# Four subtractions per pair of weight blocks, moved from VectorE to GpSimd in a Strassen-type MLP of a two-layer decoder trunk

## The chip, the cores and the metric

The kernel runs on 1 core of one Trainium2 chip. The metric is the device time of one execution in microseconds, as the median of 3 runs.

## What is computed

The reference is a decoder trunk with two layers over 1024 positions and 1024 channels, all in float32. Each layer has a mixer (a gated recurrence with a state-space layer in layer 0, latent attention in layer 1) and then a gated MLP with a short causal convolution. The change lies in the MLP:

```python
def conv_ffn(hn, w_in, conv_w, conv_b, w_out):
    a, u = jnp.split(hn @ w_in, 2, axis=-1)
    a = lax.conv_general_dilated(a, conv_w[:, None, :], window_strides=(1,),
                                 padding=[(CONV_W - 1, 0)],
                                 dimension_numbers=('NWC', 'WIO', 'NWC'),
                                 feature_group_count=D_FF) + conv_b
    return (jax.nn.silu(a) * u) @ w_out

for layer in range(DEPTH):          # DEPTH = 2
    ...                             # the mixer
    h = h + conv_ffn(rmsnorm(h, norm_ffn_g[layer]), ffn_w_in[layer], ffn_conv_w[layer],
                     ffn_conv_b[layer], ffn_w_out[layer])
```

D_FF is 2816, so `w_out` is 2816 x 1024.

## The kernel before

Both products of the MLP use a Strassen-type scheme: seven products of blocks where a plain product needs eight, paid for by sums of blocks. Each float32 product is made of three matmuls on a high and a low part of its operands (`mm3`, lines 161 to 165). `split` (lines 128 to 132) makes the two parts: ScalarE copies the high one, VectorE subtracts it from the source.

**Up-projection** (`ffn`, lines 823 to 1114). The 2816 columns come in 22 blocks of 128, f = 0 to 21; each is a `Pair` (of a block of the gate and one of the value). Per pair there are seven products, run in the order a11, s2, a12, s3, s1, a22, s4 (line 1071), each of 12 matmuls. They go into three PSUM banks X, Y and Z. The products s2, s3 and a22 go one after the other into Y, and between two of them VectorE reads Y: line 915 after s2, line 919 after s3, line 929 after a22. Line 936 reads Z after s4. GpSimd makes the sums s1 to s4 of the weights (lines 884 to 890), adds the upper half of the convolution's input (line 902) and multiplies half of the result (line 938). ScalarE copies p1 and p5 out of the banks (lines 909 and 924). The convolution (lines 1122 and 1124) is on VectorE and its silu on ScalarE (line 1125). The loads of the weights are issued three steps ahead (`LOOK`, `prep`), from SyncE's queue.

**Sums for the down-projection.** After every second pair (`tail`, line 934), two kinds of small jobs are appended to a list, `later`. `row_sums` (lines 956 to 974) makes four sums of the MLP's rows for the pair. `weight_sums` (lines 976 to 992) makes four sums of the quarters of two blocks of 128 rows of `w_out`: it loads the two blocks (line 982), waits three jobs, subtracts four times (line 987), and after each subtraction stores the result in the DRAM tile `t_dram` (line 988). `TURNS` (line 46) says how many such turns follow which pair: one after pairs 5, 7, 11, 15 and 19, two after 9, 13 and 17, so 11 per layer. Both kinds of jobs work in the same two buffers, `homes()` (lines 950 to 954). One job is taken from the list after each product, two if more than 14 are left (lines 1100 to 1102). The down-projection (`down`) reads `t_dram` (line 1158).

The order of the instructions on each engine is not written out by hand: a planner sets it from modelled durations when the program is built. Only TensorE's order in the two projections is fixed, by `issue_after` (lines 862 and 1173). Each engine works through its own queue in order, so that an instruction that waits holds all that stand behind it in that queue.

Of the kernel before, what the change touches and what calls it, by code (L numbers as in the profile page):

```python
# [17 lines left out]
ALU = mybir.AluOpType  # L18
# [39 lines left out]
class Trunk:  # L58
# [764 lines left out]
    def ffn(self, L, h, pool, final=None):  # L823
# [3 lines left out]
        V, G, ACT = nc.vector, nc.gpsimd, nc.scalar  # L827
# [122 lines left out]
        def homes():  # L950
            return (
                self.const.tile([P, S], F32, tag="gain", name="q1", bufs=1),
                self.w.tile([P, S], F32, tag=f"wlo{WBUFS - 1}", name="q2", bufs=1),
            )
# [21 lines left out]
        def weight_sums(q):  # L976

            x = []

            def load():  # L980
                for i, y in enumerate(homes()):
                    nc.sync.dma_start(out=y, in_=w_out[(2 * q + i) * P:(2 * q + i + 1) * P])
                    x.extend((y[:, lo], y[:, hi]))

            def step(i, out, a, b):
                def go():
                    V.tensor_tensor(out=x[out], in0=x[a], in1=x[b], op=ALU.subtract)
                    nc.sync.dma_start(out=t_dram[q, i], in_=x[out])
                return go

            wait = lambda: None
            return [load, wait, wait, wait, step(0, 0, 1, 0), step(2, 1, 3, 1), step(1, 3, 3, 0), step(3, 2, 2, 3), wait]
# [692 lines left out]
```

## Time and profile before

| | us |
|---|---|
| median of 3 runs | 2261.92 (2260.53 to 2264.37) |
| the profiled execution | 2260.85 |
| its span, first to last instruction | 2259.1 |
| TensorE busy | 2192.1 (97%) |
| VectorE busy | 1661.3 (74%) |
| ScalarE busy | 926.0 (41%) |
| GpSimd busy | 560.8 (25%) |
| SyncE's DMA queue, share of 16 engines | 41.1% |

Busy time is the time in which an engine has an instruction at work. In the rows PE is TensorE, DVE VectorE, ACT ScalarE, POOL GpSimd and SP SyncE. The name behind an arrow or in front of it is the tile of the program: `q<-q` is an operation from the buffers q1 and q2 of `homes()` into them, `au` is a bank X, Y or Z, `op` an operand split into two parts. L987 is line 987. "A <- B" in a list of waits says that A stood idle until B was done.

### The profile page before, as it was taken

How to read it: one execution, taken by the hardware profiler on the slowest of the kernel's cores; microseconds unless marked ns; L12 is line 12 of the kernel's file. 1: busy time of each engine (PE TensorE's matmuls, PEld its weight loads, DVE VectorE, ACT ScalarE, POOL GpSimd, SP SyncE). 2: the span in 40 equal slices, each digit the busy share in tenths (PEclk: the TensorE clock that was granted, in tenths of full speed). 3: DMA queues.
4: the chain of work that ended last, by engine and by line, in shares of the span. 5: the costliest groups of instructions: out<-in, count | busy, mean ns of one | idle time of the engine just before them, and what ended most of it. 6: DMA issues, size and time to landing. Idle time of an engine off the chain costs nothing. (4 is left out here: it accounts for less than half of the span.)

```text
span 2259.1 us, 30081 instructions
## 1 busy us (share of the span) xinstructions
PE 2192.1 (97%) x10681; PEld 1802.8 (80%) x10681; DVE 1661.3 (74%) x2749; ACT 926.0 (41%) x1564; POOL 560.8 (25%) x509
## 2 busy tenths in 40 slices
PE   7999999999999999999999999999999999999998
PEld 6777887877887777888898888888778877778886
DVE  6778896689777778754657777756887777788546
ACT  4444544443332333433433555545433332334432
POOL 0476510025444443100001000000354434431000
PEclk9999999999999999999999999999999999999999
DMA  6433323413445545875401000242134454558642
GB/s 194 137 98 91 102 86 111 149 38 122 135 139 199 165 157 193 308 248 162 145 11 46 31 27 32 88 167 94 38 122 135 150 191 163 168 200 312 233 149 84
DMA packets 257214, 306.18 MB, mean 136 GB/s; under 512 B 35680, under 2 KB 159784, under 8 KB 256552
## 3 DMA queue, kind: packets, MB, share of 16 engines
q1 hardware_dynamic: 257064, 304.26, 41.1%
q8 instruction: 84, 1.38, 0.3%
q14 instruction: 66, 0.54, 0.1%
HBM read 223.06 MB, written 79.95 MB: 134 GB/s over the span
## 5 line engine op out<-in xcount | busy, mean ns | idle before, releaser
L163 PE MATMUL au<-bt,op 128*128 128x512 f32 x704 | 282.8, 402 | 25.5 <-DVE p L915 12.7
L164 PE MATMUL au<-bt,op 128*128 128x512 f32 x704 | 279.6, 397 | 1.7 <-DVE bt L132 1.7
L165 PE MATMUL au<-bt,op 128*128 128x512 f32 x704 | 279.5, 397 | 0.0
L132 DVE TENSOR_TENSOR unit<-row,unit 128x1024 fp32r<-128x1024 f32 x154 | 184.9, 1234 | 128.7 <-ACT unit L131 125.4
L131 ACT ACTIVATE op<-raw 128x512 fp32r<-128x512 f32 x260 | 162.2, 627 | 277.7 <-POOL raw L888 130.5
L132 DVE TENSOR_TENSOR op<-raw,op 128x512 fp32r<-128x512 f32 x260 | 229.4, 884 | 56.1 <-ACT op L131 55.2
L131 ACT ACTIVATE unit<-row 128x1024 fp32r<-128x1024 f32 x154 | 155.4, 1053 | 211.0 <-PE row L165 122.8
L164 PE MATMUL row<-unit 128*128 128x512 f32 x616 | 240.4, 390 | 0.4 <-DVE unit L132 0.3
L165 PE MATMUL row<-unit 128*128 128x512 f32 x616 | 240.1, 390 | 0.0
L163 PE MATMUL row<-unit 128*128 128x512 f32 x616 | 240.0, 390 | 0.0
L165 PE MATMUL au<-b,op 128*128 128x512 f32 x528 | 208.7, 395 | 1.1 <-DVE op L132 1.1
L163 PE MATMUL au<-b,op 128*128 128x512 f32 x528 | 208.5, 395 | 0.0
L164 PE MATMUL au<-b,op 128*128 128x512 f32 x528 | 208.4, 395 | 0.0
L163 PEld LDWEIGHTS au<-bt,op 128*128 128x128 f32 x704 | 133.0, 189 | 70.2 <-DVE p L915 21.2
L132 DVE TENSOR_TENSOR wlo<-raw,whi 128x1024 fp32r<-128x1024 f32 (+4 forms) x99 | 117.4, 1188 | 60.9 <-ACT whi L131 60.2
L164 PEld LDWEIGHTS au<-bt,op 128*128 128x128 f32 x704 | 133.3, 189 | 33.0 <-DVE bt L132 2.6
L165 PEld LDWEIGHTS au<-bt,op 128*128 128x128 f32 x704 | 133.2, 189 | 32.1
L131 ACT ACTIVATE whi<-raw 128x1024 fp32r<-128x1024 f32 (+4 forms) x99 | 97.0, 981 | 113.4 <-PE row L165 42.2
L164 PEld LDWEIGHTS row<-unit 128*128 128x128 f32 x616 | 115.7, 188 | 25.7 <-DVE unit L132 1.5
L163 PEld LDWEIGHTS row<-unit 128*128 128x128 f32 x616 | 115.6, 188 | 24.3
L165 PEld LDWEIGHTS row<-unit 128*128 128x128 f32 x616 | 115.6, 188 | 24.2
L884 POOL TENSOR_TENSOR s<-raw 128x512 f32<-128x512 f32 x44 | 62.5, 1422 | 256.6 <-DMA raw<-in_ffn_w_in 255.2
(599 smaller groups left out, 5070.1 us busy)
## 6 DMA issues: line engine op xcount, KB each, us to landing
raw<-in_ffn_w_in SPq DMA_DIRECT2D x176, 256.0 KB
row<-g_dram SPq DMA_DIRECT2D x154, 256.0 KB
g_dram<-q SPq DMA_DIRECT2D x88, 256.0 KB
q<-in_ffn_w_out SPq DMA_DIRECT2D x44, 512.0 KB
t_dram<-q SPq DMA_DIRECT2D x88, 256.0 KB
row<-t_dram SPq DMA_DIRECT2D x88, 256.0 KB
raw<-in_even_w_in SPq DMA_DIRECT2D x40, 512.0 KB
g_dram<-ct SPq DMA_DIRECT2D x66, 256.0 KB
```

The source lines that it names most:

```text
L131: nc.scalar.activation(hi, src, AF.Copy)
L132: nc.vector.tensor_tensor(out=lo, in0=src, in1=hi.bitcast(F32), op=ALU.subtract)
L163: mm(out, l[0], r[0], start=start, stop=False, **how)
L164: mm(out, l[0], r[1], start=False, stop=False, **how)
L165: return mm(out, l[1], r[0], start=False, stop=stop, **how)
L884: tt(out=s.s1, in0=p("a21"), in1=p("a22"), op=ALU.add)
```

## The change

The four subtractions of `weight_sums` are issued on GpSimd (`G`) instead of VectorE (`V`). Their operands, the loads before them and the stores behind them stay as they are.

```diff
--- before.py
+++ after.py
@@ -984,7 +984,7 @@
 
             def step(i, out, a, b):
                 def go():
-                    V.tensor_tensor(out=x[out], in0=x[a], in1=x[b], op=ALU.subtract)
+                    G.tensor_tensor(out=x[out], in0=x[a], in1=x[b], op=ALU.subtract)
                     nc.sync.dma_start(out=t_dram[q, i], in_=x[out])
                 return go
 
```

## Rows read from the trace of the kernel before

**Rows 1.** The page's first part: busy us (share of the span) and instructions
```profile
PE 2192.1 (97%) x10681; PEld 1802.8 (80%) x10681; DVE 1661.3 (74%) x2749; ACT 926.0 (41%) x1564; POOL 560.8 (25%) x509
```

**Rows 2.** TensorE's waits, 600 to 904 us: us in total, times, longest us
```profile
PE au L163 <- DVE p L915: 5.0, 7, 1.6
PE au L163 <- DVE u L919: 2.4, 2, 1.3
```

**Rows 3.** TensorE's waits, 1730 to 2045 us
```profile
PE au L163 <- DVE p L915: 5.8, 8, 2.2
PE au L163 <- DVE u L919: 2.4, 3, 1.2
```

**Rows 4.** Busy us (xinstructions) of PE, PEld, DVE, ACT, POOL in a stretch
```profile
600.00:904.00 304.00, 296.40 (x1261) 235.43 (x1259) 233.41 (x297) 97.04 (x152) 125.44 (x103) 1.00 0.52 172
```

**Rows 5.** VectorE's groups, 600 to 904 us: busy us, mean ns, idle before
```profile
L132 DVE TENSOR_TENSOR op<-raw,op 128x512 fp32r<-128x512 f32 x88 | 77.2, 877 | 20.1 <-ACT op L131 19.7
...
L987 DVE TENSOR_TENSOR q<-q,q 128x512 f32<-128x512 f32 x22 | 19.2, 870 | 6.7 <-DMA q<-in_ffn_w_out 6.6
L987 DVE TENSOR_TENSOR q<-q 128x512 f32<-128x512 f32 x22 | 15.5, 702 | 29.1 <-DMA q<-in_ffn_w_out 29.1
L1122 DVE TENSOR_SCALAR ct<-ax,taps 128x1024 f32<-128x1024 f32 x15 | 14.0, 932 | 0.0
L965 DVE TENSOR_TENSOR q<-ct 128x512 f32<-128x512 f32 x14 | 12.9, 919 | 0.0
```

**Rows 6.** VectorE's waits: 600 to 904 us, then 1730 to 2045 us
```profile
DVE q L987 <- DMA q<-in_ffn_w_out: 35.7, 14, 5.1
...
DVE q L987 <- DMA q<-in_ffn_w_out: 40.6, 16, 4.0
```

**Rows 7.** VectorE's timeline before a stall: start us, us, instruction, [idle before it]
```profile
764.88 0.79 DVE L987 TENSOR_TENSOR q<-q 128x512 f32<-128x512 f32 x1 [3.53 <-DMA q<-in_ffn_w_out]
...
774.83 0.69 DVE L987 TENSOR_TENSOR q<-q 128x512 f32<-128x512 f32 x1 [0.73 <-DMA q<-in_ffn_w_out]
775.44 1.77 DVE L132 TENSOR_TENSOR op<-raw,op 128x512 fp32r<-128x512 f32 x1
777.13 0.67 DVE L915 TENSOR_TENSOR p<-p,au 128x512 f32<-128x512 f32 x1
```

**Rows 8.** TensorE's timeline: a product without a stall, and three with one
```profile
616.72 0.40 PE L163 MATMUL au<-bt,op 128*128 128x512 f32 x1
...
702.12 0.47 PE L163 MATMUL au<-bt,op 128*128 128x512 f32 x1 [1.26 <-DVE u L919]
...
777.86 0.50 PE L163 MATMUL au<-bt,op 128*128 128x512 f32 x1 [1.59 <-DVE p L915]
...
1993.92 0.48 PE L163 MATMUL au<-bt,op 128*128 128x512 f32 x1 [1.24 <-DVE u L919]
```

**Rows 9.** One of GpSimd's groups, 600 to 904 us
```profile
L902 POOL TENSOR_TENSOR ax<-u,p 128x512 f32<-128x512 f32 x15 | 21.2, 1414 | 2.2 <-ACT p L924 2.0
```

**Rows 10.** GpSimd's timeline in a single turn
```profile
603.63 1.30 POOL L902 TENSOR_TENSOR ax<-u,p 128x512 f32<-128x512 f32 x1
```

**Rows 11.** VectorE's timeline in the same turn
```profile
605.08 0.69 DVE L987 TENSOR_TENSOR q<-q 128x512 f32<-128x512 f32 x1 [2.63 <-DMA q<-in_ffn_w_out]
...
609.20 0.80 DVE L1122 TENSOR_SCALAR ct<-ax,taps 128x1024 f32<-128x1024 f32 x1
...
614.72 0.68 DVE L915 TENSOR_TENSOR p<-p,au 128x512 f32<-128x512 f32 x1
```

**Rows 12.** Another of VectorE's waits, 600 to 904 us
```profile
DVE ct L937 <- ACT ct L1125: 3.2, 7, 0.5
```

**Rows 13.** VectorE's timeline behind a doubled turn
```profile
704.23 1.78 DVE L965 TENSOR_TENSOR q<-ct 128x512 f32<-128x512 f32 x1
...
709.58 0.80 DVE L1122 TENSOR_SCALAR ct<-ax,taps 128x1024 f32<-128x1024 f32 x1
```

**Rows 14.** GpSimd's timeline behind the same turn
```profile
705.42 1.75 POOL L902 TENSOR_TENSOR ax<-u,p 128x512 f32<-128x512 f32 x1
```

## What I expect of the change

> **What bounds the kernel now.** I read the shares first: TensorE is busy for 2192.1 of 2259.1 us, so only TensorE's idle time can be won back [rows 1]. Next I asked where that idle time lies in the stretches where the moved line 987 runs: 600 to 904 us (layer 0) and 1730 to 2045 us (layer 1). TensorE waits there for two lines of VectorE: 5.0 + 2.4 us in layer 0 and 5.8 + 2.4 us in layer 1, 15.6 us in 20 waits [rows 2, 3]. These lines, 915 and 919, add a finished product out of the bank Y, and the next product into Y can't start before them. One other product, 12 matmuls, covers each of them. VectorE isn't full: 233.4 of 304 us [rows 4]. It is late because of what it does just before. In the stalled case TensorE starts 0.06 us after line 915 ends (777.13 + 0.67 = 777.80, then 777.86) and had idled 1.59 us [rows 7, 8]. Ahead of line 915 VectorE stood still twice in front of a subtraction of line 987, whose weight quarters had not landed: 3.53 us at 764.88 and 0.73 us at 774.83 [rows 7]. These stops sum to 35.7 us in layer 0 and 40.6 us in layer 1 [rows 6]. So the stalls come from a queue: a transfer holds a subtraction that nobody needs soon, and behind it in VectorE's order stand the adds that TensorE needs within one product's time, some 2.9 us (304 us over 15 pairs of seven products [rows 4, 5]).
>
> **Removed from VectorE.** 88 subtractions, 44 a layer: 19.2 + 15.5 = 34.7 us a layer [rows 5], and the stops of 35.7 and 40.6 us [rows 6]. Together it is 70.4 us of VectorE's time in layer 0, in which 7.4 us of TensorE's stalls arise, so 0.105 us of stall per us of VectorE's delay.
>
> **Added to GpSimd.** Its line 902 takes 1.41 us on average in the layer-0 stretch [rows 9]; that is also my price for a moved one, as the shape (128x512 f32, two SBUF inputs) is the same. 44 x 1.41 = 62 us bring GpSimd from 125.4 [rows 4] to 187 of 304 us, so it has the room. The chain from the landed quarters to the last store gets longer by up to 4 x (1.41 - 0.69) = 2.9 us. Nobody reads t_dram before the down-projection, so that by itself costs nothing.
>
> **Queued behind the moved wait.** The wait for the load now stands in GpSimd's queue. Behind it come line 902, which completes the conv's input, line 890 (the sum s4 of the next pair, wanted four products later, some 11 us), line 938 and the next pair's sums. Only line 902 is close to TensorE: the conv, line 1122, needs it, and lines 936 and 915 follow the conv on VectorE. In the turn at 605 us line 902 ended at 603.63 + 1.30 = 604.93 and the conv began at 609.20 [rows 10, 11], 4.3 us of cover. If that cover goes, the conv stops VectorE just as the load did.
>
> **Queued behind the moved stores.** SyncE's queue issues the four stores of a turn in order, each after its subtraction, and loads of ffn_w_in for a later pair stand behind them. They slip by at most the 2.9 us. The sums s1 and s3 want them some five products later (a pair of seven takes 304 / 15 = 20.3 us [rows 4, 5], so 14 us), and I cost this at nothing; without that cover s1 would hold up GpSimd's queue, line 902 in it.
>
> **Contention.** GpSimd's and VectorE's two-input operations hold each other up. Line 132 on `raw` took 877 ns on average in the stretch, and up to 1.77 us, beside 0.69 us undisturbed; line 1122 took 932 ns, and 0.80 us undisturbed [rows 5, 7, 11]. The excess of these two, 88 x 0.19 + 15 x 0.13 = 18.7 us, over 88 GpSimd operations (103 less 15 small memsets [rows 4]) gives 0.21 us each; with line 965 some 0.25 us. The moved 44 then hand 11 us a layer back to VectorE. Bounds: 0, and the longest excess of one, 1.77 - 0.69 = 1.08 us, 47.5 us a layer. I take 11, as it is a mean over this very mixture. At 0.105 that is 1.2 us of stall a layer, 2.4 us in all.
>
> The Trainium skill speaks against the change here. Its Perfetto Trace Analysis (Optimizing Scalar/DVE Operations) says that the two engines share an SBUF read port, so that moving work between them might not help; SBUF — State Buffer (SBUF: two separate sides) makes it an exclusive lock, where the loser blocks for the whole instruction. The 1.77 us beside 0.69 us fit a block. By the rule the 47.5 us would stand in the sum instead of 11; what that gives is the second rival below.
>
> **The sum.** Thirteen of the twenty stalls are longer than 0.4 us (14.2 us together; the first and the last stand in [rows 8]); they lie in turns or right behind them. I let these go, and keep the seven of some 0.2 us (1.4 us): VectorE waits seven times in layer 0 for the silu behind the conv [rows 12], and they follow it. Given back: 2.4 us for contention, and something in the turns that run doubled (three a layer, pairs 9, 13 and 17). There GpSimd's queue is dense. Line 902 ended at 705.42 + 1.75 = 707.17 and the conv began at 709.58 [rows 13, 14]. Three subtractions ahead, 4.2 us, push the conv by 4.2 - 2.4 = 1.8 us. A doubled turn may cost 0 to 1.8 us; I take 0.5, near the lower end, because VectorE is freed of three subtractions (2.1 us) there: six times, 3 us. Net: 14.2 - 2.4 - 3 = 8.8, say 9 us. The profiled execution took 2260.85 us (span 2259.1), 1.07 us less than the median of the runs, 2261.92. It would become 2252; against the median, **2253 us**. Elsewhere no row is touched, and I add nothing.
>
> **Rivals.** The time can resolve about 0.2%, 4.5 us either way: faster means below 2257.4, slower above 2266.4.
>
> All stalls of the two stretches go, the small ones too: 2261.9 - 15.6 = 2246. For it: VectorE is freed of 70 us and regains 11. Against it: the waits for the silu are not touched by the change. Chance 0.15.
>
> The port decides: each moved operation blocks VectorE for 1.08 us, and the load's wait passes to the conv through line 902. VectorE then carries 47.5 - 34.7 = 12.8 us a layer more than now; at 0.105 that is 1.3 us of stall a layer, 2264.6, no change. For it: excesses of 1.08 us do occur [rows 7]. Against it: the mean is a quarter of that. It is the rule of the Trainium skill named above, at its hardest. Chance 0.12.
>
> A new wait: in the doubled turns the row sums, line 965, write into the same two buffers and must wait for the last stores. The first one starts at 704.23 [rows 13] with nothing to spare. GpSimd's longer chain makes it up to 2.9 us later, on VectorE, in front of line 929: six times 2 us give 12 us back, of 14.2 minus 2.4. 2262, no change. Chance 0.12.
>
> Slower: GpSimd runs the subtractions ahead of line 902. In the turn at 605 the load lands just before 605.08; four of 1.41 us end at 610.7 and line 902 at 612.1. The conv starts 2.9 us later than now, 0.6 us are saved as a subtraction between conv and line 915 is gone, and line 915 now has 1.26 us to spare (615.40 to 616.72, less 0.06) [rows 8, 11]: a stall of 1.0 us in each of 22 turns, 23 us, less the 14.2 that go, +9: 2271. It decides where line 902 ends later than 611.06: in this turn from the fourth subtraction ahead, where the load lands 2.5 us later from the second. For it: the order is planned ahead, on transfers taken as shorter than they are, or VectorE wouldn't stop 30 times. Against it: line 902 belongs to earlier work. Chance 0.14.
>
> **How the numbers follow.** The forecast (8.8 us, with 5 to 13 by the bounds of the doubled turns and of contention) has 0.47. Faster: 0.47 + 0.15 = 0.62; same: 0.12 + 0.12 = 0.24; slower: 0.14. The range runs from a little under the case that all stalls go, 2244, to the near half of the slower case, 2268; it leaves out some 0.12.
>
> **What would show it.** Right: line 987 on GpSimd at some 1.4 us; the waits of VectorE for the load gone; TensorE's waits for lines 915 and 919 in the two stretches down from 15.6 us to about 7; line 132 on `raw` at some 1.0 us. Wrong: line 1122 waiting for line 902 (slower), line 965 waiting for a store of t_dram (new wait), line 132 near 1.3 us (port). The prediction falls altogether if TensorE's order changes outside the two stretches by more than these 9 us.

## The result, and the profile after

The changed kernel takes 2293.92 us (median of 4 runs, 2289.92 to 2295.59), the kernel before 2261.79 (4 runs, 2260.53 to 2264.37): a recorded ratio of 1.0134, 95% interval 1.0119 to 1.0149 (the two medians alone give 1.0142). It is slower by 32 us, where 9 us less were forecast. The profiled execution of after took 2295.21 us with a span of 2293.2, 34.1 us more than that of before.

The page's first part, after (busy us, share of the span, instructions):

```profile
PE 2205.1 (96%) x10681; PEld 1812.6 (79%) x10681; DVE 1675.5 (73%) x2661; ACT 925.6 (40%) x1564; POOL 704.8 (31%) x597
```

Against [rows 1], 88 instructions left VectorE, and yet its busy time rose from 1661.3 to 1675.5 us. GpSimd took 144 us more, 1.64 us for each of the 88 subtractions, and TensorE is busy for 13.0 us more and idle for 21.1 us more.

TensorE's waits, after, 600 to 904 us and then 1730 to 2080 us (us in total, times, longest us):

```profile
PE au L163 <- DVE p L915: 18.6, 10, 3.3
...
PE au L163 <- DVE p L915: 16.3, 9, 3.0
PE row L164 <- DVE unit L132: 1.8, 1, 1.8
```

The stalls for line 919 are gone from these stretches [rows 2, 3], but those for line 915 grew from 10.8 to 34.9 us: together from 15.6 to 34.9 us. There are 19 of them instead of 20, and they are on average more than twice as long (1.84 us instead of 0.78).

**Why line 915 is late.** VectorE's groups, after, 604 to 920 us (the same pairs as 600 to 904 us before; busy us, mean ns, idle before):

```profile
L132 DVE TENSOR_TENSOR op<-raw,op 128x512 fp32r<-128x512 f32 x88 | 85.5, 977 | 38.8 <-ACT op L131 38.3
L1124 DVE SCALAR_TENSOR_TENSOR ct<-ax,taps,ct 128x1024 f32<-128x1024 f32 x30 | 54.0, 1799 | 0.4
L1122 DVE TENSOR_SCALAR ct<-ax,taps 128x1024 f32<-128x1024 f32 x15 | 22.8, 1517 | 2.4 <-POOL ax L902 2.4
L132 DVE TENSOR_TENSOR op<-s,op 128x512 fp32r<-128x512 f32 x15 | 14.3, 952 | 0.0
```

Two groups of before, 600 to 904 us, that no step of the prediction looked at:

```profile
L1124 DVE SCALAR_TENSOR_TENSOR ct<-ax,taps,ct 128x1024 f32<-128x1024 f32 x30 | 38.3, 1277 | 0.2
...
L132 DVE TENSOR_TENSOR op<-s,op 128x512 fp32r<-128x512 f32 x15 | 10.2, 681 | 0.0
```

The convolution's line 1124 took 1277 ns before, as good as undisturbed, and takes 1799 ns after: 30 x 0.52 = 15.7 us. Line 1122 takes 22.8 instead of 14.0 us and line 132 on raw 85.5 instead of 77.2 [rows 5], line 132 on s 14.3 instead of 10.2. That is 36.9 us more; line 965 takes 1.6 us less. The 44 moved operations thus hand VectorE some 35 us a layer, 0.8 us each, and it had been freed of 34.7 us [rows 5]. The moved operations pay too:

```profile
L987 POOL TENSOR_TENSOR q<-q,q 128x512 f32<-128x512 f32 x22 | 39.0, 1773 | 8.2 <-DMA q<-in_ffn_w_out 7.5
L987 POOL TENSOR_TENSOR q<-q 128x512 f32<-128x512 f32 x22 | 34.9, 1586 | 8.1 <-DMA q<-in_ffn_w_out 6.1 <-DVE op L132 1.2
```

That is GpSimd's part of the same stretch of after, with a mean of 1.68 us. The waits for the load have moved there, and they are shorter (13.6 us instead of 35.7, [rows 6]).

**One turn.** VectorE in the turn of [rows 10, 11], before, behind line 1122 (start us, us, instruction, [idle before it]):

```profile
611.12 1.27 DVE L1124 SCALAR_TENSOR_TENSOR ct<-ax,taps,ct 128x1024 f32<-128x1024 f32 x1
612.32 0.68 DVE L132 TENSOR_TENSOR op<-s,op 128x512 fp32r<-128x512 f32 x1
612.92 1.27 DVE L1124 SCALAR_TENSOR_TENSOR ct<-ax,taps,ct 128x1024 f32<-128x1024 f32 x1
```

VectorE in the same turn, after:

```profile
612.14 1.78 DVE L1122 TENSOR_SCALAR ct<-ax,taps 128x1024 f32<-128x1024 f32 x1
613.96 2.20 DVE L1124 SCALAR_TENSOR_TENSOR ct<-ax,taps,ct 128x1024 f32<-128x1024 f32 x1
...
616.68 1.19 DVE L132 TENSOR_TENSOR op<-s,op 128x512 fp32r<-128x512 f32 x1
617.79 2.30 DVE L1124 SCALAR_TENSOR_TENSOR ct<-ax,taps,ct 128x1024 f32<-128x1024 f32 x1
...
621.22 0.69 DVE L937 TENSOR_TENSOR ct<-ct,au 128x512 f32<-128x512 f32 x1 [0.53 <-ACT ct L1125]
621.82 0.68 DVE L915 TENSOR_TENSOR p<-p,au 128x512 f32<-128x512 f32 x1
```

GpSimd in the same turn, after:

```profile
610.38 1.29 POOL L902 TENSOR_TENSOR ax<-u,p 128x512 f32<-128x512 f32 x1
611.63 1.74 POOL L890 TENSOR_TENSOR raw<-raw 128x512 f32<-128x512 f32 x1
613.33 3.98 POOL L987 TENSOR_TENSOR q<-q,q 128x512 f32<-128x512 f32 x2
617.39 1.61 POOL L987 TENSOR_TENSOR q<-q 128x512 f32<-128x512 f32 x1
```

And TensorE, after:

```profile
622.56 0.50 PE L163 MATMUL au<-bt,op 128*128 128x512 f32 x1 [1.65 <-DVE p L915]
```

From the start of the conv to the end of line 915 before needed 6.20 us (609.20 to 615.40, [rows 11]) and after needs 10.36 (612.14 to 622.50). Each of four operations (line 1122, line 1124 twice, line 132 on s) meets a GpSimd operation and is 0.51 to 1.03 us longer, 3.4 us in all. Three meet moved subtractions; line 1122 meets line 890, which had ended before the conv in before (606.45 + 1.68) and is now behind a subtraction and line 902. Then comes a thing that the diff doesn't show: the planner has turned two instructions round. In the turns of before, line 915 stands ahead of line 937 (the product with the silu's result); in after line 937 stands ahead in all 14 pairs of this stretch; here it waits 0.53 us for the silu and takes 0.60 us. A subtraction that stood between conv and line 915 is gone (0.6 us). That makes 3.9 of the 4.16 us. TensorE comes to this product 4.19 us later than before (at 622.56 - 1.65 instead of 616.72, [rows 8]) and the conv starts only 2.94 us later, a gain of 1.25; line 915 had 1.26 us to spare: 4.16 - 1.25 - 1.26 = 1.65 us, the stall.

**What a stall brings on top.** TensorE behind the longest stall of after:

```profile
813.84 0.79 PE L163 MATMUL au<-bt,op 128*128 128x512 f32 x1 [3.26 <-DVE p L915]
814.43 0.63 PE L164 MATMUL au<-bt,op 128*128 128x512 f32 x1
814.86 0.63 PE L165 MATMUL au<-bt,op 128*128 128x512 f32 x1
```

The 20 us around it, then the part with the slow matmuls (busy us of PE, PEld, DVE, ACT, POOL; granted clock; DMA share; GB/s):

```profile
800.00:820.00 20.00, 16.74 (x61) 13.05 (x60) 15.31 (x18) 4.55 (x8) 10.74 (x9) 0.83 0.46 157
814.00:819.50 5.50, 5.50 (x13) 4.29 (x14) 3.02 (x6) 0.08 (x1) 1.62 (x2) 0.50 0.97 329
```

The matmuls start every 0.43 us instead of every 0.23 us: TensorE's clock is at the lower of its two levels (granted share 0.50, 1.2 instead of 2.4 GHz) from the first matmul behind the stall, and comes back after twelve more. Such a stretch, of 6 to 13 slow matmuls, follows stalls of 1.87, 2.51, 2.72, 3.03 and 3.26 us; it doesn't follow stalls of 2.07 and 2.21 us. Between 440 us and the end, 63 matmuls of after start 0.43 us apart, and 18 of before: 45 x 0.194 us (0.427 less 0.233) = 8.7 us.

**The split of the 34.1 us.** In the whole run the stalls for lines 915 and 919 went from 12.7 + 8.3 to 37.5 + 2.3 us: 18.8. The clock took 8.7, the wait in front of the down-projections 1.5 (0.3 before). Another 4.05 us lie ahead of the first changed instruction (480.56 us before, 484.61 after); that point also varies in executions of other kernels with the same instructions up to there (481.8 us in e3, 484.8 in e8), so it is taken as no effect of the change. The sum is 33.

### The profile page after: what moved, and what is told of

Its sections match the earlier page's. It is cut to its first block, busy times and chain, and to the rows that moved or that the text cites. A ratio compares the mean times of both kernels' runs of the same rounds, so it can differ in the third digit from the quotient of the medians.

```text
span 2293.2 us, 30085 instructions
## 1 busy us (share of the span) xinstructions
PE 2205.1 (96%) x10681; PEld 1812.6 (79%) x10681; DVE 1675.5 (73%) x2661; ACT 925.6 (40%) x1564; POOL 704.8 (31%) x597
## 5 line engine op out<-in xcount | busy, mean ns | idle before, releaser
L163 PE MATMUL au<-bt,op 128*128 128x512 f32 x704 | 287.3, 408 | 44.2 <-DVE p L915 37.5
L132 DVE TENSOR_TENSOR op<-raw,op 128x512 fp32r<-128x512 f32 x260 | 247.5, 957 | 92.7 <-ACT op L131 91.6
L164 PE MATMUL au<-bt,op 128*128 128x512 f32 x704 | 283.7, 403 | 1.8 <-DVE bt L132 1.8
L165 PE MATMUL au<-bt,op 128*128 128x512 f32 x704 | 283.1, 402 | 0.0
L163 PEld LDWEIGHTS au<-bt,op 128*128 128x128 f32 x704 | 135.7, 193 | 89.5 <-DVE p L915 48.5
L164 PEld LDWEIGHTS au<-bt,op 128*128 128x128 f32 x704 | 135.9, 193 | 33.9 <-DVE bt L132 2.6
L165 PEld LDWEIGHTS au<-bt,op 128*128 128x128 f32 x704 | 135.7, 193 | 33.0
L1124 DVE SCALAR_TENSOR_TENSOR ct<-ax,taps,ct 128x1024 f32<-128x1024 f32 x88 | 146.7, 1667 | 1.2
L164 PEld LDWEIGHTS row<-unit 128*128 128x128 f32 x616 | 115.7, 188 | 26.8 <-DVE unit L132 2.6
L163 PEld LDWEIGHTS row<-unit 128*128 128x128 f32 x616 | 115.6, 188 | 24.4
```

The costliest lines, as they stand in the source:

```text
L132: nc.vector.tensor_tensor(out=lo, in0=src, in1=hi.bitcast(F32), op=ALU.subtract)
L163: mm(out, l[0], r[0], start=start, stop=False, **how)
L164: mm(out, l[0], r[1], start=False, stop=False, **how)
L165: return mm(out, l[1], r[0], start=False, stop=stop, **how)
L1124: nc.vector.scalar_tensor_tensor(out=t, in0=at(s), scalar=col(s), in1=t, op0=ALU.mult, op1=ALU.add)
```

## The experiments

Theory, once the two traces were compared: GpSimd's subtractions block VectorE's operations in the conv, which stands on the way to line 915 (the port). Rivals: the planner's new order, 937 ahead of 915, does it by itself; or GpSimd's queue does it (lines 902, 888). Each ratio below is against runs of the kernel before on the same chip (medians there of 2265.8 to 2267.0 us).

**e1: the changed kernel with line 915 ahead of line 937.** An order without a wait: line 937 may only be issued behind line 915 of the next pair (`behind`, defined further up, tells the planner so).

```diff
-                V.tensor_tensor(out=p.p16, in0=p.p1, in1=p.Y, op=ALU.add)
+                add = V.tensor_tensor(out=p.p16, in0=p.p1, in1=p.Y, op=ALU.add); behind(add)
...
-            V.tensor_tensor(out=ct[:, lo], in0=ct[:, lo], in1=p.X, op=ALU.mult)
+            halves.append(V.tensor_tensor(out=ct[:, lo], in0=ct[:, lo], in1=p.X, op=ALU.mult))
```

> The changed kernel with one order turned round: VectorE's add out of bank Y (line 915) is put ahead of its product with the silu (line 937) in every pair. After the change the planner had 937 ahead of 915 in the turns too. Theory port (the moved subtractions stand beside the conv, lines 1122 and 1124, and hold it up by some 3.4 us; the order adds 1.2 us on top): stalls of line 915 fall from some 1.8 us by about 1.2 us each, not to nothing; about 2268 us. Theory order (937 ahead of 915 is the whole cause): the stalls go, 2245 to 2255 us. Theory queue (line 902 behind the first subtraction on GpSimd delays the conv): nothing changes, 2285 to 2294 us.

Measured: 2291.73 us, ratio 1.0110 (1.0092 to 1.0127). TensorE's waits, 600 to 690 us (the two single turns behind pairs 5 and 7), then 600 to 920 us:

```profile
PE au L163 <- DVE p L915: 0.4, 1, 0.4
...
PE au L163 <- DVE p L915: 8.8, 6, 2.1
PE au L163 <- ACT p L924: 2.9, 3, 1.9
```

In the single turns the stalls fall from 1.4 to 1.65 us to at most 0.4, though the conv is as slow as in after (line 1124 at 1767 ns). In the doubled turns 1.85 to 2.06 us remain, and waits for line 924 are new. Over the whole run the stalls for line 915 fall from 37.5 to 18.0 us, but 12.8 us of waits for line 924 and 2.0 us more for line 919 take most of that back, and the interval overlaps that of after. So the order has a part in the stalls for line 915; forced on every pair, it costs three quarters as much elsewhere, and its share of the loss can't be read from this total.

**e2: the kernel before with line 937 ahead of line 915.**

```diff
-                V.tensor_tensor(out=p.p16, in0=p.p1, in1=p.Y, op=ALU.add)
+                with tc.issue_after(halves[0].ins) if halves else nullcontext(): V.tensor_tensor(out=p.p16, in0=p.p1, in1=p.Y, op=ALU.add)
...
-            V.tensor_tensor(out=ct[:, lo], in0=ct[:, lo], in1=p.X, op=ALU.mult)
+            halves[:] = [V.tensor_tensor(out=ct[:, lo], in0=ct[:, lo], in1=p.X, op=ALU.mult)]
```

> The kernel before, subtractions on VectorE, with line 937 put ahead of line 915 in every pair, as the planner did after the change. Theory order: this alone brings the loss, 2285 to 2294 us. Theory port: line 915 comes 1.1 us later and has 1.26 us to spare, so little happens: 2260 to 2268 us. Theory queue: no change, 2260 to 2264 us.

Measured: 2304.33 us, ratio 1.0171 (1.0156 to 1.0186), a miss as a total. The order is forced on every pair, on the first ones too, where the planner had line 915 well ahead: there, where no turn runs, it stalls TensorE for 5.83 us at 527.79 and 2.99 us at 546.90, and 11 us of waits at the down-projection's start are new. In the two single turns, 600 to 690 us, TensorE doesn't wait for line 915 at all. So the order alone does no harm in these two turns. In the single turns behind pairs 11 and 15 it does, by some 1.3 us each (the stalls go from 0.43 to 1.75 us and from 1.64 to 2.88 us): the stalls of before show that no time was left to spare there. This total says nothing on the change.

With before and after, e1 and e2 make a square for the single turns of 600 to 690 us: subtractions on VectorE, either order: no stall; on GpSimd with 915 ahead: 0 to 0.4 us; on GpSimd with 937 ahead: 1.4 to 1.65 us. In these turns it takes both to use up the 1.26 us and more.

**e3: GpSimd writes the same buffers, but reads nothing.** Two fills with zeros stand in place of each subtraction; the sums of the weight quarters are left out.

```diff
-                    G.tensor_tensor(out=x[out], in0=x[a], in1=x[b], op=ALU.subtract)
+                    G.memset(x[out], 0.0); G.memset(x[out], 0.0)
```

> The changed kernel with each of the 88 subtractions on GpSimd replaced by two memsets of the same output (no reads from SBUF, about the same time on GpSimd, the same place in its queue and the same stores; the sums of the weight quarters are left out). Theory port: lines 1122 and 1124 go back to some 0.8 and 1.28 us, and most of the stalls go: 2250 to 2265 us. Theory order: the loss stays, 2285 to 2294 us. Theory queue: it stays too, as the memsets wait for the load ahead of line 902.

Measured: 2273.32 us, ratio 1.0027 (1.0013 to 1.0042). Four fifths of the loss are gone, and no stall is left from 600 to 690 us, with line 937 still ahead of 915. Line 1124 is at 1521 ns (1799 in after, 1277 before), line 132 on s at 682 and on raw at 896. The rise of line 1124 isn't the fills': its 8 slow ones of 30 (2.18 to 2.19 us) all begin beside line 890, which reads, and the other 22 take 1.27 to 1.29 us. VectorE and GpSimd in the turn at 609 us:

```profile
609.51 2.18 DVE L1124 SCALAR_TENSOR_TENSOR ct<-ax,taps,ct 128x1024 f32<-128x1024 f32 x1
...
612.22 0.68 DVE L132 TENSOR_TENSOR op<-s,op 128x512 fp32r<-128x512 f32 x1
```

```profile
608.89 1.72 POOL L890 TENSOR_TENSOR raw<-raw 128x512 f32<-128x512 f32 x1
610.56 1.92 POOL L987 MEMSET q<- 128x512 f32 x4
```

What remains is another mechanism, in a doubled turn. GpSimd, ScalarE and TensorE there:

```profile
702.43 1.92 POOL L987 MEMSET q<- 128x512 f32 x4 [2.59 <-DMA q<-in_ffn_w_out]
704.32 1.26 POOL L888 TENSOR_TENSOR raw<-s,raw 128x512 f32<-128x512 f32 x1
```

```profile
705.62 0.63 ACT L131 ACTIVATE op<-raw 128x512 fp32r<-128x512 f32 x1 [9.19 <-POOL raw L888]
706.15 0.58 ACT L924 ACTIVATE p<-au 128x512 f32<-128x512 f32 x1
```

```profile
706.78 0.50 PE L163 MATMUL au<-b,op 128*128 128x512 f32 x1 [2.49 <-ACT p L924]
```

This is the queue rival: line 888 (the sum s2) stands behind the second load of a doubled turn in GpSimd's queue, ScalarE's split of s2 waits for it, and line 924, which empties a bank, stands behind that split. It gives 14.9 us of waits here. In after TensorE shows no wait for line 924, presumably because the stalls for line 915 have put it behind already. A caution: two memsets take 0.96 us and a subtraction takes 1.68, so e3 shortens GpSimd's work as well as taking its reads away.

**e4 and e12: the kernel before, with extra subtractions on GpSimd beside the conv.** Three per turn in e4, one in e12. They read `ax`, and their result is not used.

```diff
-                self.conv(p.ct, p.ax, taps, p.f, slice(0, S))
+                self.conv(p.ct, p.ax, taps, p.f, slice(0, S)); [G.tensor_tensor(out=p.s1, in0=kn(p.ax[:, 2:2 + HALF]), in1=kn(p.ax[:, 2 + HALF:]), op=ALU.subtract) for _ in range(3 * (p.f - 1 in TURNS))]
```

> The kernel before, its subtractions on VectorE, and beside the conv of each of the 8 pairs per layer behind which a turn follows, three more subtractions on GpSimd that read the conv's input and write to a tile no longer needed. It is the disputed cost by itself: VectorE's order, loads and stores stay as they were. Theory port: line 1124 rises to 1.7 us or more in these pairs and line 915 stalls there by 1.5 to 3 us: 16 pairs, 2285 to 2300 us with what the clock adds. Theory order and theory queue: 2260 to 2266 us.

> The kernel before with one more subtraction on GpSimd beside the conv of the 8 pairs per layer, in place of three. Three delayed line 915 by some 5.3 us (a stall of 4.0 us, and 1.26 us to spare), 1.75 us each. One then gives 0.5 us of stall in each of 16 pairs, 8 us, with little lowered clock: a ratio of 1.003 to 1.006. If a single collision is hidden by the time to spare: 1.000 to 1.002.

Measured: e4 2330.89 us, ratio 1.0285 (1.0267 to 1.0303), where 2285 to 2300 us was expected; e12 2301.44 us, ratio 1.0160 (1.0144 to 1.0177), where 1.003 to 1.006 was expected. Both keep 915 ahead of 937 in the turns and leave line 987 on VectorE, and both stall TensorE for line 915, by 57.2 and 42.0 us (12.7 before). But e12 isn't the single collision that it was meant to be. GpSimd, VectorE and TensorE in its first turn:

```profile
610.67 1.73 POOL L930 TENSOR_TENSOR s<-ax 128x512 f32<-128x512 f32 x1
612.48 1.62 POOL L884 TENSOR_TENSOR s<-raw 128x512 f32<-128x512 f32 x1
614.18 1.62 POOL L886 TENSOR_TENSOR raw<-raw 128x512 f32<-128x512 f32 x1
```

```profile
611.18 1.77 DVE L132 TENSOR_TENSOR op<-raw,op 128x512 fp32r<-128x512 f32 x1
612.88 1.77 DVE L1122 TENSOR_SCALAR ct<-ax,taps 128x1024 f32<-128x1024 f32 x1
614.57 1.78 DVE L987 TENSOR_TENSOR q<-q 128x512 f32<-128x512 f32 x1
```

```profile
621.20 0.50 PE L163 MATMUL au<-bt,op 128*128 128x512 f32 x1 [2.09 <-DVE p L915]
```

The extra operation (line 930 there) writes the buffer of s1 and held lines 884 and 886 back until it was done, so three GpSimd operations came in front of the conv and beside its start. Each made one VectorE operation some 1.0 to 1.1 us longer (0.69 to 1.77, 0.80 to 1.77, 0.68 to 1.78 us): 3.15 us against 1.26 to spare leave 1.9, and 2.09 were measured. It shows the price of one full collision, and that collisions just in front of the conv and behind its start stall TensorE without a change of order and without a load in GpSimd's queue.

**e5 and e6: no doubled turns,** in the changed kernel (e5) and in the kernel before (e6). The idea was that after loses its time in the dense doubled turns.

```diff
-TURNS = {5: 1, 7: 1, 9: 2, 11: 1, 13: 2, 15: 1, 17: 2, 19: 1}
+TURNS = {1: 1, 3: 1, 5: 1, 7: 1, 9: 1, 11: 1, 13: 1, 15: 1, 17: 1, 19: 1, 21: 1}
```

> The changed kernel with the eleven turns of a layer spread one by one behind every odd pair (1 to 21), none doubled. In the trace after the change the second turn of a pair costs 2.5 to 3.3 us at line 915 and nearly all of the stretches at the lower clock follow it; a single one costs some 1.5 us. Theory port: each single turn still collides with its conv, 22 x 1.5 us of stalls and hardly any lowered clock: 2275 to 2283 us. Theory doubled (the loss is that of the doubled turns, where GpSimd's queue is dense): 2255 to 2265 us.

> The kernel before with the same single turns, subtractions on VectorE: the partner of the run above. In the trace of before the two single turns ahead of the first doubled one have no stall, so that the stalls of 15.6 us come from the doubled ones: 2248 to 2256 us if that holds, 2260 to 2264 us if the load's wait on VectorE costs as much in single turns, more if the early pairs, which are dense, can't take a turn.

Measured: e5 2316.03 us, ratio 1.0216 (1.0201 to 1.0232); e6 2279.64 us, ratio 1.0054 (1.0039 to 1.0069). Both lose some 20 us at the start of the down-projections, where the last turn gets in its way (waits for line 131, 20.3 and 20.6 us), so that only the stretch before is to be compared. In e5 seven of seven turns from 600 to 904 us still stall TensorE, 1.43 to 2.3 us each: doubling isn't the cause in the changed kernel. e6 says something else. TensorE's waits, then VectorE's, e6, 600 to 904 us:

```profile
PE au L163 <- DVE p L915: 1.0, 2, 0.7
```

```profile
DVE q L987 <- DMA q<-in_ffn_w_out: 33.1, 9, 4.5
```

VectorE stops for the load for 33.1 us in 9 times, as long in sum as in before (35.7 in 14, [rows 6]), and TensorE waits for 1.0 us instead of 7.4 [rows 2]. In a turn that stands alone the stops cost next to nothing. The stalls of before come with its doubled turns: they lie in them or in a turn close behind one, the longest of layer 0 (1.64 us at 819.73) in the single turn behind pair 15. Where a stop stands is what differs: all nine of e6 stand ahead of line 929, in front of the conv, while six of the 14 of before, all in doubled turns, stand behind the conv's start, ahead of line 915 (693.0, 774.8, 857.8 us) or line 919 (698.8, 780.4, 863.4), and four of the six have a stall right behind them (at 777.86, 859.76, 702.12 and 866.80).

**e7: the kernel before with e1's order.** Its edit is that of e1.

> The kernel before with line 915 ahead of line 937 in every pair. Seven of its stalls, 0.2 us each, and some of the others follow a product with the silu put ahead of the add. Theory: 3 to 6 us faster, 2256 to 2259 us beside 2262. If the order is of no account on VectorE: no change.

Measured: 2275.39 us, ratio 1.0047 (1.0030 to 1.0063). Waits for line 915 go from 12.7 to 14.7 us and those for line 919 from 8.3 to 14.2. The planner's own order is the best of the three for before.

**e8: the kernel before with the subtractions five jobs behind the load instead of three.**

```diff
-            return [load, wait, wait, wait, step(0, 0, 1, 0), step(2, 1, 3, 1), step(1, 3, 3, 0), step(3, 2, 2, 3), wait]
+            return [load, wait, wait, wait, wait, wait, step(0, 0, 1, 0), step(2, 1, 3, 1), step(1, 3, 3, 0), step(3, 2, 2, 3)]
```

> The kernel before with two more empty jobs between the load and the first subtraction of a turn (and the empty one at the end dropped), so that the planner sees the subtractions later. If its order follows the list, VectorE no longer stands still for the load (76 us in 30 stops before), and most of the 15.6 us of stalls go: 2248 to 2255 us. If the planner places them by its own model of the load's landing, the stops stay, and the time too.

Measured: 2267.24 us, ratio 1.0002 (0.9992 to 1.0011). The stops remain (42.2 us in 600 to 904 us). This fits a planner that puts the subtractions where its model has the load landed, wherever they stand in the list; the trace doesn't show its reasons.

**e9, e10 and e11: turns spread out,** nine single and one doubled (e9, the kernel before; e11, the changed kernel with e1's order), or seven single and two doubled (e10, the kernel before: doubled behind pairs 9 and 15, single behind 3, 5, 7, 11, 13, 17 and 19). The turns of e9 and e11:

```diff
-TURNS = {5: 1, 7: 1, 9: 2, 11: 1, 13: 2, 15: 1, 17: 2, 19: 1}
+TURNS = {1: 1, 3: 1, 5: 1, 7: 1, 9: 1, 11: 2, 13: 1, 15: 1, 17: 1, 19: 1}
```

> The kernel before, subtractions on VectorE, with its turns behind pairs 1 to 19, all single but the one behind pair 11, and none behind the last pair, which in the run with eleven single turns ran into the down-projection. With single turns the two stretches kept 2.4 of 15.6 us of stalls at lines 915 and 919, though VectorE stood still for the load as long as before (78 us). If the doubled turns made the stalls, this one is faster than before by 5 to 12 us, a ratio of 0.995 to 0.998. If the early pairs can't take a turn: no change.

> The kernel before with turns behind pairs 3 to 19, those behind 9 and 15 doubled: two doubled ones in place of three, and none in the earliest pairs. By the count of doubled turns a third of the 15 us goes, a ratio of some 0.998; no change if they aren't the cause.

> The changed kernel, subtractions on GpSimd, with the turns of e9 and with line 915 ahead of line 937. In the first single turns the stall was 1.4 to 1.7 us with GpSimd's collision and the order that the planner gave, and 0 to 0.4 us with either alone. If the two work together only, nearly all stalls of the single turns go, and what is left is the doubled turn and the lowered clock: a ratio of 0.998 to 1.004. If the collision costs by itself: 1.008 or more.

Measured: e9 2259.90 us, ratio 0.9975 (0.9966 to 0.9984); e10 2262.11 us, ratio 0.9984 (0.9975 to 0.9993); e11 2272.74 us, ratio 1.0033 (1.0022 to 1.0044). e9 beats both kernels. TensorE's waits in it, 600 to 904 us:

```profile
PE au L163 <- DVE p L915: 1.9, 4, 1.1
PE au L163 <- DVE u L919: 1.2, 1, 1.2
```

3.1 us instead of 7.4, with VectorE's stops for the load as long as before (36.1 us). Ahead of the two stretches (440 to 600 and 1600 to 1730 us) the same waits grow, from 5.4 to 12.1 us, where turns now stand behind pairs 1 and 3, so that over the whole run they fall by 2.2 us only (21.0 to 18.8). e11 gets back three quarters of what the change loses, by turns that meet less and by the order, but with line 1124 at 1769 ns it stays behind the kernel before, and 0.6% behind e9, which has the same turns, the subtractions on VectorE and the planner's own order.

## Why the prediction was wrong

**The first step that failed: what an operation beside GpSimd costs (contention).** The prediction took the mean excess of the mixture of before, 0.25 us for each GpSimd operation, and called 1.08 us a bound. Measured are 0.8 us on average, and 0.5 to 1.0 us wherever one falls beside the conv. The mean of before was low because GpSimd's operations there fell mostly beside other work: line 1124 was undisturbed at 1277 ns. The moved ones fall beside it. So the term was mis-sized by a factor of three, 35 us a layer instead of 11. The rule of the Trainium skill that stood against the change (Perfetto Trace Analysis, Optimizing Scalar/DVE Operations; SBUF — State Buffer, SBUF: two separate sides) was the better guide. The traces agree that an operation of one engine holds one of the other's: in e12 the held operations take 0.97 to 1.10 us longer, most of the 1.30 us that a GpSimd operation takes alone [rows 10]. The trace of after adds that GpSimd loses as well: 1.68 us on average.

**The second: 0.105 us of stall per us of VectorE's delay.** Even with the full 47.5 us, the port rival came out at 2264.6, because delay was taken as spread over the stretch. Two runs contradict it. In e6, 33.1 us of stops give 1.0 us of stall; in e12's first turn 3.15 us of collisions give 2.09. The delay counts where it lies close ahead of line 915, just in front of the conv or behind its start, beyond some 1.26 us to spare; ahead of line 929, where the stops of e6 stand, most of it is covered. The right sum was at hand in the prediction's own slower rival (what stands between conv and line 915, against 1.26 us), but it was made there only for subtractions ahead of line 902.

**The third: the stalls of before were put down to the wrong thing.** "So the stalls come from a queue" is half right. The example was taken from a doubled turn [rows 7, 8], and e6 and e9 show that the same stops in single turns are covered. Only what the doubling brings was to be won back there, and e9 wins part of it without the change.

**Not in the prediction at all:** that the planner would turn lines 915 and 937 round (a term of some 1.1 us in each turn), and that TensorE's clock is lower behind some of the longer stalls (8.7 us).

**The rivals.** The slower one forecast 2271 by subtractions ahead of line 902. They do stand there: one in the turn at 605 us, and VectorE waits for line 902. But this is small, as the waits of VectorE from 600 to 940 us in after show, the new wait of line 965 among them:

```profile
DVE ct L937 <- ACT ct L1125: 6.6, 14, 0.5
DVE q L965 <- DMA t_dram<-q: 5.1, 3, 1.7
DVE ct L1122 <- POOL ax L902: 2.4, 2, 1.2
```

With 5.2 and 3.6 us in layer 1, the waits for the stores and for line 902 together are 16 us of VectorE's time. The sign was the rival's, the mechanism was not. Line 937 now waits for the silu in 14 pairs instead of 7 [rows 12].

**Right:** VectorE's waits for the load are gone, the stalls at line 919 are gone from the stretches, GpSimd has room, and line 132 on raw stands at 0.98 us (some 1.0 was forecast). This last was taken as a mark of the mild case; the mark was wrong, since the conv was where to look. A subtraction on GpSimd takes 1.68 instead of 1.41 us.

**Open.** How much of the loss each collision makes alone wasn't isolated (e12 brought three at once), nor was the share of the new order. A version with the subtractions on GpSimd kept clear of the conv wasn't tried. And that the new order follows from GpSimd's modelled times is inferred; the planner's reasons are not in the trace.

## What to carry to other kernels

Before you move an operation to an engine with room, look at what it will run beside, and price it by the full collision seen in the trace (here about 1 us on VectorE and 0.4 us on GpSimd), not by a mean over a mixture in which the collisions fell elsewhere. Count a delay where it lies on the way to the bound engine, against the time to spare there: 33 us of stops cost 1 us in e6, and 3.15 us of collisions cost 2.09 us in one turn of e12. A change of engine also lets a planner reorder what stands around it, so compare the order of the instructions near the bound before you believe the sum.

## What the runs showed of the hardware

- An operation of VectorE with one tensor input isn't safe either: line 1122, a TENSOR_SCALAR of 128x1024, goes from 0.80 to 1.78 us beside a subtraction on GpSimd.
- An operation of VectorE that takes one of its inputs from a bank wasn't held: in after, 600 to 925 us, all 15 of line 915 and all 15 of line 929 ran beside a GpSimd operation that reads SBUF, and the longest took 0.69 us.
- A GpSimd operation that only writes held nothing up here: in e3 line 132 on s stays at 682 ns beside the fills (952 beside subtractions in after), and every slow line 1124 of its turns lies beside line 890.
- TensorE's clock is at its lower level behind stalls of 2.5 to 3.3 us, and behind one of 1.87 us, but not behind stalls of 2.07 and 2.21 us: the length of the stall alone doesn't settle it. Such a stall is followed by 6 to 13 slow matmuls and so costs 1.2 to 2.5 us more than its own length (at 0.194 us each).
